# Weight gradient on one core: X of the first slices on SP's queue and slice 0 of G on ACT's, an uneven rounding split, and a last bank in two pieces

## The chip, the cores and the metric

The kernel runs on one core of a Trainium2 chip. The metric is device time in microseconds (us). One profiled execution of each kernel gives a span (first to last instruction), which lies about 1.8 us below the device time of the same execution. PE is TensorE (matmul), PEld its weight loads, DVE VectorE, ACT ScalarE, POOL GpSimd, SP SyncE.

## The reference

```python
batch, m, k, n = 16, 512, 1024, 768
# input: (16, 512, 1024) fp32, grad_output: (16, 512, 768) fp32
grad_weight = np.einsum('bmk,bmn->kn', input, grad_output)
```

With batch and m joined this is one product X^T G: 8192 rows are summed, in 64 slices of 128 rows.

## The kernel before

GpSimd's queue loads X and G slice by slice and casts them to bf16 on the way. The first slices can't wait for that: SP and ACT load slice 0 of G and slices 0 and 1 of X as fp32, and DVE and ACT round them to bf16. G's 768 columns are used in two parts: the "wide" 512 columns as moving operand (steps A and B of the order, four banks each), and the "narrow" 256 columns as stationary operand (steps N). A bank is one accumulator of 128 x 512 fp32 that matmuls write; in the order below the number is the slice up to which a step works, and "!" means that its banks are then copied or added out. Ten long and two short matmuls on constants keep TensorE busy until the data are there.

```python
ORDER = ("A1! B1 N1 B2! N2 A2 N3! ... A50! B50! N64!").split()
WARMUP = [512] * 10 + [128] * 2
...
nc.sync.dma_start(out=gf[:, 0:NA], in_=G[0:P, 0:NA])       # wide G, 256 KB
nc.scalar.dma_start(out=xf[0], in_=X[0:P, :])              # X slice 0, 512 KB
nc.sync.dma_start(out=gf[:, NA:N], in_=G[0:P, NA:N])       # narrow G, 128 KB
nc.scalar.dma_start(out=xf[1], in_=X[P : 2 * P, :])        # X slice 1, 512 KB
...
round_by("DVE", g0, gf, 0, 256)
round_by("ACT", g0, gf, 256, NA)
round_by("DVE", xs[0], xf[0], 0, P)
round_by("ACT", xs[0], xf[0], 2 * P, 4 * P)
round_by("DVE", xs[0], xf[0], P, 2 * P)
...                                              # the rest of X slice 0
def add_slice(part, i, s, first, last):
    ...
    if part.first:
        copy_out(dst, bank, i)                   # even i on DVE, odd on ACT
        if s == 0 and i == 0:
            round_by("DVE", g0, gf, NA, N)       # the narrow G
...
for k in range(KS):                              # the last slices, bank by bank
    pieces = [(0, NA)] if k < KS - 1 else [(0, 256), (256, 384), (384, NA)]
    for c0, c1 in pieces:
        ...                                      # 14 matmuls, then the add
        W = NB if k < 6 else c1 - c0
        for c in range(c0, c1, W):
            nc.sync.dma_start(out=OUT[:, k, c : c + W], in_=acc[:, k, c : c + W])
```

## Time and profile before

| | before |
|---|---|
| device time, median of 3 runs | 176.05 us (175.82 to 176.11) |
| span of the profiled run | 174.3 us |
| PE busy | 97% |
| first real weight load | 5.32 us |
| first N weight load | 6.98 us |
| last add | 171.50 us |

A line of a timeline reads: start (us), length (us), engine, line of the program, operation, what it writes and reads, form, count; in brackets the idle time before it and what ended it. A weight load normally runs one matmul ahead. The lines that carry this part are in the prediction.

### The profile page before, as it was taken

Reading aid. Unit: us, or ns where it says so; the run is one execution under the profiler, and the core shown is the slowest. Engines: PE = TensorE matmul, PEld = TensorE weight load, DVE = VectorE, ACT = ScalarE, POOL = GpSimd, SP = SyncE. Lnnn points to the kernel's source line nnn. Section 1 sums busy time; section 2 is a strip of 40 time slices with the busy share of each in tenths; the row PEclk is TensorE's granted clock in tenths of the full one; section 3 lists DMA queues with packets and bytes.
Section 4 is the critical chain, followed back from the end, with each engine's and each line's share of the span. In section 5 each row is a group of like instructions: output and inputs, shape, how many; then the busy total and the mean of one; then the engine's idle time right before and its main releaser. Section 6 shows DMA issues by size and latency. Waiting matters only on the chain.

```text
span 174.3 us, 2013 instructions
## 1 busy us (share of the span) xinstructions
PE 169.9 (97%) x793; PEld 78.4 (45%) x808; DVE 61.3 (35%) x103; ACT 6.2 (4%) x12; POOL 66.7 (38%) x129
## 2 busy tenths in 40 slices
PE   8999999999999999999999999999999999999993
PEld 3444444444444444444444444444444444444463
DVE  0655582883940039300000662200560003931122
ACT  2640000000000000000000000000000000000000
POOL 7444434444444444444444444444274200000000
PEclk9999999999999999999999999999999999999999
DMA  5999999999999999999999999999999990085623
GB/s 192 276 208 209 207 209 208 208 208 209 207 208 209 207 208 210 207 209 209 206 209 208 208 210 207 207 209 208 207 209 209 207 202 11 0 190 160 170 86 120
DMA packets 25048, 33.35 MB, mean 191 GB/s; under 512 B 6480, under 2 KB 16592, under 8 KB 25040
## 3 DMA queue, kind: packets, MB, share of 16 engines
q0 software_dynamic: 18000, 28.65, 89.9%
q10 hardware_dynamic: 4448, 2.10, 4.7%
q1 hardware_dynamic: 2592, 2.49, 4.2%
q8 instruction: 6, 0.10, 0.2%
q14 instruction: 2, 0.02, 0.0%
HBM read 58.72 MB, written 3.15 MB: 355 GB/s over the span
## 4 chain that ended last, share of the span: by engine, by line
PE 97%; issue 0%; DVE 0%
PE bank L127 63%; PE bank L134 32%; PE bank L81 3%; DVE acc L118 0%
## 5 line engine op out<-in xcount | busy, mean ns | idle before, releaser
L127 PE MATMUL bank<-gt,xt 128*128 128x512 bf16 (+2 forms) x515 | 108.3, 367 | 0.5
L127 PEld LDWEIGHTS <-xt 128*128 128x128 bf16 x524 | 50.2, 98 | 57.2
L118 DVE TENSOR_TENSOR acc<-bank,acc 128x512 f32<-128x512 f32 (+2 forms) x62 | 37.9, 667 | 73.4 <-PE bank L127 72.9
L134 PE MATMUL bank<-xt,gt 128*128 128x512 bf16 x242 | 54.8, 379 | 0.3
L97 POOL DMA_DIRECT2D xt<-in_input_dram x62 | 33.1, 533 | 38.7 <-DMA xt<-in_input_dram 36.5
L92 POOL DMA_DIRECT2D gt<-in_grad_output_dram x63 | 33.8, 536 | 31.2 <-DMA gt<-in_grad_output_dram 24.9
L134 PEld LDWEIGHTS <-gt 128*128 128x128 bf16 x252 | 24.6, 98 | 29.7
L118 DVE TENSOR_TENSOR acct<-bank,acct 128x512 f32<-128x512 f32 x24 | 15.7, 682 | 30.0 <-PE bank L134 29.9
L81 PE MATMUL bank<-const-bfloat16-1.0 128*128 128x512 bf16 (+1 forms) x12 | 4.6, 574 | 0.8 <-PEq L263 0.8
L81 PEld LDWEIGHTS <-const-bfloat16-1.0 128*128 128x128 bf16 x12 | 1.6, 140 | 3.5 <-issue 3.5
L122 DVE COPY acc<-bank 128x512 f32<-128x512 f32 x4 | 2.7, 687 | 1.0 <-PE bank L127 1.0
L180 DVE STREAM_TRANSPOSE turned<-acct 128x512 f32<-128x512 f32 x4 | 2.9, 715 | 0.1
L127 PEld LDWEIGHTS <-x 128*128 128x128 bf16 x16 | 1.6, 98 | 1.9 <-DVE x L107 0.2
L107 DVE CAST g<-gf 128x256 bf16<-128x256 f32 x2 | 0.6, 290 | 4.7 <-DMA gf<-in_grad_output_dram 4.7
L124 ACT COPY acc<-bank 128x512 f32<-128x512 f32 x4 | 2.1, 589 | 1.3 <-PE bank L127 1.3
L127 PE MATMUL bank<-gt,x 128*128 128x512 bf16 x8 | 2.1, 379 | 0.0
L127 PE MATMUL bank<-g,x 128*128 128x512 bf16 x8 | 2.0, 398 | 0.0
L122 DVE COPY acct<-bank 128x512 f32<-128x512 f32 x2 | 1.3, 686 | 1.3 <-PE bank L134 1.3
L107 ACT CAST x<-xf 128x256 bf16<-128x256 f32 x4 | 1.4, 409 | 0.0
L107 ACT ACT_TABLE_LOAD x1 | 1.3, 1283 | 1.7 <-PEq L263 1.7
L124 ACT COPY acct<-bank 128x512 f32<-128x512 f32 x2 | 1.1, 588 | 1.5 <-PE bank L134 1.5
L107 DVE CAST x<-xf 128x256 bf16<-128x256 f32 (+1 forms) x5 | 1.0, 260 | 0.0
(8 smaller groups left out, 3.3 us busy)
## 6 DMA issues: line engine op xcount, KB each, us to landing
xt<-in_input_dram POOLq DMA_DIRECT2D x62, 256.0 KB, 8.5
gt<-in_grad_output_dram POOLq DMA_DIRECT2D x63, 192.0 KB, 8.5
out_dram<-acc SPq DMA_DIRECT2D x13, 128.0 KB, 2.7
xf<-in_input_dram ACTq DMA_DIRECT2D x2, 512.0 KB, 5.1
out_dram<-turned ACTq DMA_DIRECT2D x4, 256.0 KB, 3.4
gf<-in_grad_output_dram SPq DMA_DIRECT2D x1, 256.0 KB, 3.9
out_dram<-acc SPq DMA_DIRECT2D x1, 256.0 KB, 2.0
gf<-in_grad_output_dram SPq DMA_DIRECT2D x1, 128.0 KB, 4.7
```

What stands on the lines that cost most here:

```text
L81: nc.tensor.matmul(wps[:, 0:cols], ones, nc.const_aps.tensor(1.0, (P, cols), bf16), start=True, stop=True,)
L92: nc.gpsimd.dma_start(out=gt, in_=G[s * P : (s + 1) * P, :])
L97: nc.gpsimd.dma_start(out=xs[s], in_=X[s * P : (s + 1) * P, :])
L107: copy(out=dst[:, c0:c1], in_=src[:, c0:c1])
L118: nc.vector.tensor_add(out=dst, in0=src, in1=dst)
L122: nc.vector.tensor_copy(out=dst, in_=src)
L124: nc.scalar.copy(out=dst, in_=src)
L127: nc.tensor.matmul(bank, xs[s][:, k * P : (k + 1) * P], gwide[s][:, c0:c1], start=start, stop=stop)
L134: nc.tensor.matmul(bank, gnarrow[s].rearrange("p (r t) -> p t r", t=NT)[:, t], xs[s][:, h * NA : (h + 1) * NA], start=start, stop=stop,)
L180: nc.vector.transpose(out=turned[:, h * hb : (h + 1) * hb, :, t], in_=dst.rearrange("p (b r) -> p b r", r=SQ),)
```

## The change

Its intent: start X, the larger load, first on SP's queue; let ACT, the slower one, take no X before the first matmul but the larger piece of G; and drop 14 matmuls at the end.

```diff
-    nc.sync.dma_start(out=gf[:, 0:NA], in_=G[0:P, 0:NA])
-    nc.scalar.dma_start(out=xf[0], in_=X[0:P, :])
-    nc.sync.dma_start(out=gf[:, NA:N], in_=G[0:P, NA:N])
-    nc.scalar.dma_start(out=xf[1], in_=X[P : 2 * P, :])
+    nc.sync.dma_start(out=xf[0], in_=X[0:P, :])
+    nc.scalar.dma_start(out=gf[:, 0:NA], in_=G[0:P, 0:NA])
+    nc.sync.dma_start(out=xf[1], in_=X[P : 2 * P, :])
+    nc.scalar.dma_start(out=gf[:, NA:N], in_=G[0:P, NA:N])
...
-    round_by("DVE", g0, gf, 0, 256)
-    round_by("ACT", g0, gf, 256, NA)
+    round_by("ACT", g0, gf, 0, 288)
     round_by("DVE", xs[0], xf[0], 0, P)
+    round_by("DVE", g0, gf, 288, NA)
...
-        pieces = [(0, NA)] if k < KS - 1 else [(0, 256), (256, 384), (384, NA)]
+        pieces = [(0, NA)] if k < KS - 1 else [(0, 384), (384, NA)]
...
-            W = NB if k < 6 else c1 - c0
+            W = NB if k < KS - 1 else c1 - c0
```

## The prediction

> **What bounds the kernel now.** I read the page first: busy shares, then the chain that ended last.
>
> ```profile
> PE 169.9 (97%) x793; PEld 78.4 (45%) x808; DVE 61.3 (35%) x103; ACT 6.2 (4%) x12; POOL 66.7 (38%) x129
> ...
> PE 97%; issue 0%; DVE 0%
> ```
>
> TensorE (PE) is busy for 97% of the span and the chain of waits lies on it from start to end. So the time is: when the first real matmul starts, plus a fixed stream of matmuls, plus what follows the last one. The change touches only the first 6 us and the last 5 us of a 174.3 us span. The middle stays: the waits view has no wait of a matmul on data after the first one. Next, the timeline of the head, from 4.9 to 5.45 us (start, length, engine, line, operation, count, idle time before):
>
> ```profile
> 4.71 0.41 ACT L107 CAST g<-gf 128x256 bf16<-128x256 f32 x1 [1.76 <-DMA gf<-in_grad_output_dram]
> 4.71 0.29 DVE L107 CAST g<-gf 128x256 bf16<-128x256 f32 x1 [4.71 <-DMA gf<-in_grad_output_dram]
> 5.00 0.15 PEld L81 LDWEIGHTS <-const-bfloat16-1.0 128*128 128x128 bf16 x1 [0.28 <-issue]
> 5.04 0.71 ACT L107 CAST x<-xf 128x256 bf16<-128x256 f32 x2
> 5.04 0.56 DVE L107 CAST x<-xf 128x128 bf16<-128x128 f32 x3
> ...
> 5.32 0.10 PEld L127 LDWEIGHTS <-x 128*128 128x128 bf16 x1 [0.17 <-DVE x L107]
> 5.32 0.53 PE L127 MATMUL bank<-g,x 128*128 128x512 bf16 x1
> ```
>
> G of slice 0 is there at 4.71, X at 5.04. DVE rounds its half of G, then the first 128 columns of X, and the first real weight load comes at 5.32, after a wait of 0.17 us for that X. Is X or DVE the later one? Further down the trace a DVE rounding of 256 columns lets the next instruction start 0.20 us later (6.50 to 6.70), so DVE was free at 4.91 and stood until 5.04: **X's landing sets the first matmul**. The view of the tile xf agrees: its two loads take 4.3 and 5.8 us from issue to landing, and 0.74 + 4.3 = 5.04.
>
> How much can an earlier X give? The warm-up's weight loads stand 0.425 us apart, ten matmuls of 512 columns from 0.78 on are done issuing at 5.05, and two of 128 columns at about 0.107 us end near 5.26. The real work comes in the same queue, so it can start at most 0.06 us sooner.
>
> The tail, DVE's timeline from 168.3 us on, and SP's last line:
>
> ```profile
> 168.41 0.69 DVE L118 TENSOR_TENSOR acc<-bank,acc 128x512 f32<-128x512 f32 x1 [2.33 <-PE bank L127]
> 169.94 0.42 DVE L118 TENSOR_TENSOR acc<-bank,acc 128x256 f32<-128x256 f32 x1 [0.84 <-PE bank L127]
> 170.72 0.29 DVE L118 TENSOR_TENSOR acc<-bank,acc 128x128 f32<-128x128 f32 x1 [0.36 <-PE bank L127]
> 171.50 0.29 DVE L118 TENSOR_TENSOR acc<-bank,acc 128x128 f32<-128x128 f32 x1 [0.49 <-PE bank L127]
> ```
>
> ```profile
> 171.82 0.33 SPq L248 DMA_DIRECT2D out_dram<-acc  x1
> ```
>
> Each add starts when its bank is complete. 14 matmuls of 256 columns took 169.94 - 168.41 = 1.53 us (109.3 ns each), 14 of 128 columns 0.78 us (55.7 ns each); a bank of 512 took 168.41 - 165.39 = 3.02 us (215.7 ns each). The last store lands 1.5 us after its issue, at 173.32, and about 1.0 us of closing follows.
>
> **What the Trainium skill says.** "TensorE: Matmul & The Clock Gate", section "Back-to-back issue gap", gives N/2.4 + 2.5 ns for a warm matmul of N columns: 215.8, 109.2 and 55.8. The trace agrees to 0.1 ns; the 131 ns for N=512 that the same section quotes as sustained is not seen here. The same page, "Part 1: The HAM clock gate", says that TensorE runs at half clock until a window of about 3.4 us has been busy. The trace agrees in kind: warm-up matmuls 0.425 us apart, and the first real one starting at 5.32, the second at 5.68 (its end at 6.06 less 0.38), the rest 0.216 apart. 0.36 us for 512 columns is a mixture: t us at 1.2 and 0.36 - t at 2.4 columns per ns give t = 0.29, so the clock opened at about 5.61. "ScalarE: Activation LUTs", section "What ACT_TABLE_LOAD costs", gives 186 + 0.833 N ns for an instruction without pointer operands: 399 at 256 columns against 406 in the trace. "DMA: Bandwidth & Descriptors", section "Issuing engines are not separate DMA queues", says that the choice of issuing engine saves only sequencer time. By that the swap of queues is worth nothing. The trace disagrees a little: the DMA view for 1.8 to 2.1 us, when both loads had been issued at 0.74, shows
>
> ```profile
> q1 hardware_dynamic: 27, 0.06, 92.5%
> q10 hardware_dynamic: 2, 0.01, 19.5%
> ```
>
> q1 is SP's queue (it carries G now, and the 2 MB of the direct output at the end), q10 is ACT's. SP's load moves first, ACT's some 0.3 us later.
>
> **The change, part by part.**
>
> *Queues.* X (512 KB) goes first and G (256 KB) 0.3 us later. From the DMA view, X's 0.52 MB were through at about 4.35 and G's 0.26 MB at about 4.0; each was signalled some 0.7 us later. Between 2.1 and 3.8 us X got about 65% of what both moved (0.35 of 0.54 MB). With X alone until 2.1 us it has 0.07 MB by then and 0.454 left; at 65% it is through when both together have moved 0.70 MB, and G when they have moved 0.26/0.35 = 0.75 MB. Adding up the moved bytes window by window (0.54 MB by 3.8, 0.63 by 4.0, 0.70 by 4.2, 0.77 by 4.4) gives X through at 4.2 and G at 4.35: landings near 4.85 to 4.9 for X, 0.15 to 0.2 us sooner than now, and 4.95 for G, 0.25 later. These are estimates from those windows.
>
> *Rounding.* ACT takes G 0:288 (0.406 + 32 x 0.00083 = 0.43 us), from 4.95 to 5.38. DVE takes 128 columns of X at 4.88 (the next starts 0.14 us later, as three starts from 5.04 to 5.32 show), then G 288:512, 224 columns, between the 0.22 us of 128 and the 0.285 of 256 columns: 0.27 us, from about 5.02 to 5.29. A step from end of rounding to use costs 0.06 (5.26 to 5.32). The first matmul has both operands at about 5.44. Its weight load needs only X and is done by then, which before came after 5.32 and costs 0.10; so compare 5.44 with 5.42: **a slip of 0.02 us**, or, if X lands no sooner than now (5.04 + 0.14 + 0.27 + 0.06 = 5.51), of 0.09. All of this lies before the clock opens at about 5.61, where a lost us costs only half: 0.01 to 0.05 us. Later roundings (128 columns of X by DVE done at about 5.43, the pair by ACT near 5.8) are before their matmuls (second at 5.7, third at 5.9), though the third is close: one more slip of up to 0.1 is possible there.
>
> *Tail.* The last bank becomes 14 x (384/2.4 + 2.5 = 162.5 ns) + 14 x 55.7 = 2.275 + 0.780 = 3.055 us in place of 1.53 + 0.78 + 0.78 = 3.09: **0.035 us less**, the fixed 2.5 ns of 14 matmuls. The new add of 384 columns, between 0.425 and 0.692, is 0.56 us, from 170.69 to 171.25; the last add starts at 171.465, so DVE is free. The store of 384 columns is issued at 171.28 and holds SP for 0.33, to 171.61; the last is issued at 171.79, so SP is free too. The 192 KB need about 0.55 us at the 350 GB/s of the big stores, some 0.8 after issue, so from 172.05 to 172.6, just when the last 64 KB begin: at most 0.05 us of rub. The seventh bank's store split in two goes out at 169.13 and 169.5, long before. Last landing 173.28 to 173.33.
>
> Sum: head +0.01 to +0.05 (to +0.1 with the third matmul late), tail -0.035 to 0. Together about +0.02 us, 0.01% of 176.05. I put the time at 176.05.
>
> **Rivals.** *X on SP really frees the head.* If X and G both land before 4.8, the roundings end before the warm-up does, and the matmul starts at 5.26: 0.06 us at half clock, 0.03, plus 0.035 of the tail. For it: X has the whole queue first. Against it: both loads share the same bytes and about 400 GB/s from 3 us on. It would make 175.98. *DVE becomes the wait.* X now stands ahead of G in DVE's queue; if X lands late, G waits behind it with its data long there: 5.51 or later, some 176.1 to 176.15. *The clock opens later.* The gap between warm-up and real work grows from about 0.1 to 0.2 us. If that falls foul of the busy window, the array stays at half clock for up to 3.4 us more and loses half of that, 1.7 us: 177.7. Against it: the gap is 5% of a window that is otherwise full. *The last stores collide*: 0.05 to 0.2 us, 176.1 to 176.25; for it, 192 KB are 0.51 us ahead of the last 64 on the same queue where 64 KB were 0.78 ahead before.
>
> **Range and chances.** The first, second and fourth rivals stay within 0.2 us; the runs before span 0.29 us by themselves, more than any of these. So the range is run-to-run noise plus 0.1 on each side: 175.65 to 176.45. 2% is 3.5 us, and even the late clock reaches only half of it. Same: 0.98; faster and slower 0.01 each.
>
> **What would show it.** In the profile after: X landing at about 4.85 and G at about 4.95; the first real weight load before 5.2 and its matmul held by ACT's rounding of G, not by DVE's of X; the second matmul at 5.68 to 5.75; 14 matmuls of 384 columns 162.5 ns apart (the add of the 384 piece 2.275 us after that of the seventh bank); the last add 3.055 us after that of the seventh bank; the last landing about 1.5 us after its issue. Wrong would be: a third window at half clock, a wait of TensorE above 0.3 us in the head, or a last store that takes over 1.7 us to land.

## The result, and the profile after

The changed kernel takes **176.49 us** (median of 6 runs, 176.37 to 176.56) against 176.06 us for the kernel before (6 runs, 175.81 to 176.32). The ratio is 1.0025, 95% interval 1.0013 to 1.0038. A ratio here is the mean time of one kernel's fast runs over that of the other's of the same rounds, so it is not quite the ratio of the medians. The change is within 2%, as predicted, but 0.04 us above the range, and the loss of 0.25% is clear of noise.

The profiled span is 174.60 us against 174.27: 0.33 more. The chain that ended last of the changed kernel, its pieces between 0.7 and 7.6 us (start, length, what):

```profile
0.74 4.22 DMA gf<-in_grad_output_dram
...
4.99 0.44 ACT g L107
...
5.47 2.09 PE bank L127 x8
```

A load of G now stands on the chain where before it was TensorE alone. In this execution it is the wide G, issued at 0.74, which the first matmul needs. The head of the changed kernel, from its timeline for 4.4 to 5.5 us:

```profile
4.81 0.31 DVE L107 CAST x<-xf 128x128 bf16<-128x128 f32 x1 [4.81 <-DMA xf<-in_input_dram]
4.99 0.43 ACT L107 CAST g<-gf 128x288 bf16<-128x288 f32 x1 [2.04 <-DMA gf<-in_grad_output_dram]
4.99 0.28 DVE L107 CAST g<-gf 128x224 bf16<-128x224 f32 x1
...
5.31 0.26 PEld L127 LDWEIGHTS <-x 128*128 128x128 bf16 x2 [0.17 <-DVE g L107]
...
5.47 0.58 PE L127 MATMUL bank<-g,x 128*128 128x512 bf16 x1
```

X came at 4.81 and the wide G at 4.99; the first matmul started at 5.47, when ACT had rounded its 288 columns. So far this is what was forecast, though the first matmul of the kernel before had started at 5.32, so that the slip is 0.15 us and not 0.02. The next stretch was not forecast. First the kernel before, its timeline for 6.3 to 8.3 us:

```profile
6.50 0.28 DVE L107 CAST g<-gf 128x256 bf16<-128x256 f32 x1
6.70 0.68 DVE L122 COPY acc<-bank 128x512 f32<-128x512 f32 x1
6.98 0.75 PEld L134 LDWEIGHTS <-g 128*128 128x128 bf16 x4
...
7.85 0.53 PEld L127 LDWEIGHTS <-x 128*128 128x128 bf16 x3
```

and the same stretch of the changed kernel:

```profile
7.02 0.29 DVE L107 CAST g<-gf 128x256 bf16<-128x256 f32 x1 [0.24 <-DMA gf<-in_grad_output_dram]
7.23 0.68 DVE L122 COPY acc<-bank 128x512 f32<-128x512 f32 x1
...
7.36 0.35 PEld L134 LDWEIGHTS <-g 128*128 128x128 bf16 x3 [0.30 <-DVE g L107]
...
7.96 0.10 PEld L134 LDWEIGHTS <-g 128*128 128x128 bf16 x1 [0.26 <-issue]
8.18 0.10 PEld L127 LDWEIGHTS <-x 128*128 128x128 bf16 x1
```

The rounding of the **narrow G** waited for its load until 7.02, the first weight load made of it waited for the rounding until 7.36, and the fourth came only at 7.96, just after the end of the copy behind that rounding, 7.23 + 0.68 = 7.91. The first weight load of step B2 (a slice-1 X block) is at 8.18 against 7.85: 0.33 later. From there to the end of the span both take 166.42 us. **The whole difference of the two profiles lies before 8.2 us.**

A wait of a weight load is not yet a loss, since the load has a matmul's time to spare; the starts of the matmuls count. The N matmuls start at 7.20, 7.41, 7.63 and 7.84 before, and at 7.39, 7.61, 7.96 and 8.18 after. The first of them comes 0.21 us behind the last B1 matmul in both, so its 0.19 us are the later first matmul and the later clock (below). The third is held:

```profile
7.96 0.38 PE L134 MATMUL bank<-x,g 128*128 128x512 bf16 x1
```

By the kernel's order of banks it writes to the third bank of step A1, which DVE's copy behind the late rounding has just freed. So the late narrow G cost 0.14 of the 0.33 us in this execution; how much it costs in others, the experiments show.

Which load is late? Part 6 of each page, KB and us from issue to landing, before:

```profile
gf<-in_grad_output_dram SPq DMA_DIRECT2D x1, 256.0 KB, 3.9
...
gf<-in_grad_output_dram SPq DMA_DIRECT2D x1, 128.0 KB, 4.7
```

and after:

```profile
gf<-in_grad_output_dram ACTq DMA_DIRECT2D x1, 256.0 KB, 4.2
...
gf<-in_grad_output_dram ACTq DMA_DIRECT2D x1, 128.0 KB, 5.8
```

The wide G takes 0.3 us longer, the narrow G 1.1 us longer. The DMA view shows how they moved (queue, packets, MB, share of the 16 engines). Before, 4.0 to 4.8 us, the narrow G is on q1:

```profile
q10 hardware_dynamic: 64, 0.20, 62.2%
q1 hardware_dynamic: 119, 0.12, 41.0%
```

After, 4.4 to 6.0 us, it is on q10, beside X of slice 1 on q1:

```profile
q1 hardware_dynamic: 107, 0.42, 67.0%
...
q10 hardware_dynamic: 94, 0.10, 17.6%
```

Before, nearly all of the narrow G moved in 0.8 us; after, 0.10 MB of it took 1.6 us. In that stretch the two queues moved about equally many packets, but a packet of the view is one row, of the narrow G 1 KB and of X 4 KB. The Trainium skill, "DMA: Bandwidth & Descriptors", section "Queues, rings and completion order", says that each DMA engine takes turns between its queues packet by packet (its packets hold several descriptors, so only the equal turns can be compared). This stretch agrees: 107 packets against 94, 0.42 MB against 0.10. The stretch of before does not: there q1 moved 119 packets to q10's 64.

The packet records of the traces, in which the row size tells the loads apart, show why. Before, the narrow G's rows moved from 4.00 to 5.22 us, and they started just as X of slice 0 ran out on q10 and X of slice 1 began: from 4.2 to 4.6 us 74 of its 128 rows moved beside 20 rows of X. After, its first row moved at 4.53, when X of slice 1 was in full flow, and its last at 6.47; from 4.6 to 6.0 us 89 of its rows moved beside 85 of X. So the narrow G both started 0.5 us later and then had to take turns with longer rows. e8 below tests the sharing itself.

The tail, DVE from 168 us on, in the changed kernel:

```profile
168.74 0.69 DVE L118 TENSOR_TENSOR acc<-bank,acc 128x512 f32<-128x512 f32 x1 [2.33 <-PE bank L127]
171.02 0.56 DVE L118 TENSOR_TENSOR acc<-bank,acc 128x384 f32<-128x384 f32 x1 [1.58 <-PE bank L127]
171.80 0.29 DVE L118 TENSOR_TENSOR acc<-bank,acc 128x128 f32<-128x128 f32 x1 [0.22 <-PE bank L127]
```

From the seventh bank's add to the last one are 3.06 us in place of 3.09. But from the last add to the end of the span are 174.60 - 171.80 = 2.80, against 174.27 - 171.50 = 2.77. The tail comes out even.

### The profile page after: what moved, and what is told of

Its sections match the earlier page's. It is cut to its first block, busy times and chain, and to the rows that moved or that the text cites. A ratio compares the mean times of both kernels' runs of the same rounds, so it can differ in the third digit from the quotient of the medians.

```text
span 174.6 us, 1983 instructions
## 1 busy us (share of the span) xinstructions
PE 170.1 (97%) x779; PEld 77.6 (44%) x794; DVE 61.3 (35%) x102; ACT 6.2 (4%) x12; POOL 66.5 (38%) x129
## 4 chain that ended last, share of the span: by engine, by line
PE 95%; DMA 2%; issue 1%; ACT 0%; DVE 0%
PE bank L127 63%; PE bank L134 32%; DMA gf<-in_grad_output_dram 2%; ACT g L107 0%; DVE acc L118 0%
## 5 line engine op out<-in xcount | busy, mean ns | idle before, releaser
L127 PEld LDWEIGHTS <-xt 128*128 128x128 bf16 x510 | 49.4, 98 | 58.0
L134 PE MATMUL bank<-x,g 128*128 128x512 bf16 x4 | 1.2, 378 | 0.0
```

Source lines behind the costliest of these rows:

```text
L127: nc.tensor.matmul(bank, xs[s][:, k * P : (k + 1) * P], gwide[s][:, c0:c1], start=start, stop=stop)
L134: nc.tensor.matmul(bank, gnarrow[s].rearrange("p (r t) -> p t r", t=NT)[:, t], xs[s][:, h * NA : (h + 1) * NA], start=start, stop=stop,)
```

## The experiments

Ten kernels ran, in three groups, each group on one chip with its own runs of the kernel before. Two numbers beside the ratio are needed to read them. One is when the narrow G was there. The other is when TensorE's clock opened: nine of the twelve traces have a record of the stretch at full clock, and I give its start from the start of the span. (The PEclk row of the page shows 9 throughout and does not show this, as it counts time without such a record as full clock; the spacing of weight loads does show it, 0.42 us before and 0.216 after.) "Late" means that the trace has no such record and the loads are still 0.3 to 0.4 us apart at about 6.1. From the first B2 matmul to the end of the span all take 166.2 us (e1 0.2 more, see there), so that column is what an execution's head cost.

| kernel | narrow G there | clock opens | first N load | first B2 load | first B2 matmul | span | ratio to before (95%) | median |
|---|---|---|---|---|---|---|---|---|
| before | 5.9 | 5.63 | 6.98 | 7.85 | 8.06 | 174.27 | | 176.06 |
| after | 7.02 | 5.91 | 7.36 | 8.18 | 8.39 | 174.60 | 1.0025 (1.0013 to 1.0038) | 176.49 |
| e0_same | 6.6 | 4.80 | 6.98 | 7.80 | 8.01 | 174.20 | 1.0000 (0.9986 to 1.0015) | 176.10 |
| e1_tail | 5.8 | 3.81 | 6.86 | 7.72 | 7.93 | 174.34 | 1.0003 (0.9989 to 1.0018) | 176.08 |
| e2_queues | 7.03 | late | 7.38 | 8.19 | 8.40 | 174.60 | 1.0021 (1.0008 to 1.0034) | 176.51 |
| e3_round | 5.8 | 5.09 | 7.01 | 7.87 | 8.09 | 174.29 | 1.0005 (0.9991 to 1.0019) | 176.11 |
| e4_narrow | 5.6 | late | 7.28 | 8.14 | 8.36 | 174.58 | 0.9999 (0.9986 to 1.0013) | 176.00 |
| e5_fill | 7.36 | 4.86 | 7.71 | 8.56 | 8.73 | 174.94 | 1.0028 (1.0015 to 1.0040) | 176.53 |
| e6_gap | 5.8 | late | 7.42 | 8.28 | 8.49 | 174.70 | 1.0001 (0.9988 to 1.0013) | 175.96 |
| e7_narrow_fill | 5.5 | 4.81 | 6.84 | 7.70 | 7.92 | 174.13 | 1.0000 (0.9986 to 1.0013) | 175.92 |
| e8_x1_last | 5.0 | 5.20 | 6.78 | 8.90 | 8.90 | 175.13 | 1.0056 (1.0039 to 1.0072) | 177.00 |
| e9_copy_first | 7.18 | 3.62 | 7.53 | 8.19 | 8.40 | 174.59 | 1.0015 (1.0003 to 1.0027) | 176.34 |

Where no engine waited for the narrow G, its time is issue plus landing time. One sum explains most rows. With the narrow G there at time t, its rounding lets DVE's copy start 0.21 us later, the copy takes 0.68, the third N matmul starts 0.05 after it, and the first B2 matmul two matmuls (0.43) after that: t + 1.37 us at the earliest. The four profiles in which this copy held the third N matmul, or came to the same time as the clock did, agree: after, e0, e2 and e5 lie 1.37 to 1.38 us behind t. In the others without a wait for a load the clock and the first matmul set the time, 7.92 to 8.49.

**First group: which part of the change costs?** My theory was the late narrow G, brought by the swap of queues. The rivals were the rounding order, and the clock.

### e0_same: the kernel before, as a control

No edit.

> The kernel before, once more, as a control. Theory 'phase': the clock of TensorE opens at a time that changes from execution to execution, so this profile may show an opening away from 5.63 us by some tenths and a third weight load of real work away from 5.69. Theory 'gap': the opening is tied to what TensorE did, so it comes at 5.63 +- 0.05 again. Both: ratio 1.000 +- 0.001, span 174.3 +- 0.15.

The ratio is 1.0000. The clock opened at 4.80, 0.83 us earlier than in the first profile of the same program: the opening is a matter of chance, which speaks for "phase". The span gained only 0.07. In this execution the narrow G also happened to be late (6.6), and with the early clock it was waited for: an earlier clock shows the wait behind it. By the packet records 123 of its 128 rows had moved by 5.0 us, and the last five came one by one until 5.95.

### e1_tail: only the last bank's pieces

```diff
-        pieces = ... else [(0, 256), (256, 384), (384, NA)]
+        pieces = ... else [(0, 384), (384, NA)]
-            W = NB if k < 6 else c1 - c0
+            W = NB if k < KS - 1 else c1 - c0
```

> Only the last bank in 384 + 128 and the seventh bank's store in two. All theories: from the add of the seventh bank to the last add 3.055 us in place of 3.09, last store landing 1.5 to 1.6 us after issue, ratio 0.9998 (0.9990 to 1.0005). If the stores rub, over 1.0005.

The ratio is 1.0003, no difference that can be told. The last add came 3.06 us after the seventh bank's (168.48 to 171.54), the end of the span 2.80 after it. All seven profiles with two pieces (after, e1, e4, e5, e7, e8, e9) have 2.78 to 2.81 there, and all five with three (before, e0, e2, e3, e6) 2.75 to 2.77. So with two pieces the end comes 0.04 us later behind the last add, and the 0.035 saved on matmuls is gone again. That the last store now stands behind 192 KB is the likely reason; it was not tested alone. This profile lost another 0.2 us at 30.6 us, where PE came to a slice of X before its load did (its timeline there):

```profile
30.57 0.55 PEld L127 LDWEIGHTS <-xt 128*128 128x128 bf16 x4 [0.52 <-DMA xt<-in_input_dram]
```

### e2_queues: only the swap of the queues

The first block of the diff above, nothing else.

> Only the swap of the queues. Theory 'late narrow G' (the last third of G lands at 7.0 us, 1.1 later than before, because it now stands behind the wide G, which itself starts later, and beside X of slice 1): the rounding of the narrow G waits for its DMA until 7.0 again, the first N matmul is 0.3 later than before, span 174.55 to 174.7, ratio 1.002 to 1.003. Rival 'rounding order' (X ahead of G on DVE is what costs): narrow G waits but most of the loss is gone, ratio below 1.001.

```profile
7.03 0.30 DVE L107 CAST g<-gf 128x256 bf16<-128x256 f32 x1 [0.22 <-DMA gf<-in_grad_output_dram]
...
7.38 0.69 PEld L134 LDWEIGHTS <-g 128*128 128x128 bf16 x4 [0.17 <-DVE g L107]
```

The ratio is 1.0021, so the swap alone carries the loss. That rests on the five timed runs (176.37 to 176.57), not on this profile. The timeline again shows the wait for the narrow G, and the span is that of the changed kernel, but the clock was late here: the N matmuls start at 7.54, 7.75, 7.97 and 8.19, evenly behind those of B1. The clock alone would have given about this span, as e4's 174.58 shows, and the third N matmul's 7.97 is just when the copy set it free as well.

### e3_round: only the new rounding order

The second block of the diff alone.

> Only the unequal rounding in the new order, with X still on ACT and landing at 5.04. Theory 'late narrow G': no wait for the narrow G, but DVE rounds X at 5.04 and G after it, first matmul at about 5.5, loss 0.1 to 0.2 by itself, ratio 1.0005 to 1.0012. Rival 'rounding order': ratio 1.002 or more.

The ratio is 1.0005, not clear of 1. No engine waits for the narrow G. The first real weight load comes at 5.47, 0.15 later than before, because DVE now rounds G behind X. That is a small cost at most (an estimate: 0.15 us are 0.09% of the time, and at half clock half of that); the rival that it carries the loss falls.

**Second group: is it the narrow G or the clock?** In the profile after the clock opened at 5.91, in that of before at 5.63. I wanted to know whether the longer pause of TensorE before the first real matmul had put it off.

### e4_narrow: the changed kernel, narrow G second on SP

```diff
-    nc.sync.dma_start(out=xf[1], in_=X[P : 2 * P, :])
-    nc.scalar.dma_start(out=gf[:, NA:N], in_=G[0:P, NA:N])
+    nc.sync.dma_start(out=gf[:, NA:N], in_=G[0:P, NA:N])
+    nc.scalar.dma_start(out=xf[1], in_=X[P : 2 * P, :])
```

> The changed kernel with the narrow G second on SP and X of slice 1 second on ACT. Theory 'late narrow G': it lands near 6.0, its rounding by DVE no longer waits, the N matmuls start as soon as the eight wide ones are through, and about 0.13 us of the 0.33 us of span come back: span about 174.45, ratio to before 1.0012 to 1.002. Rival (all of the loss is the later first matmul and the clock): span 174.6, ratio 1.0025.

The ratio is 0.9999: all of the loss is gone, not the 0.13 of 0.33 us I had expected. (The 0.13 was right for the first two profiles, see the third N matmul above; in the timed runs the late narrow G costs more.) The five runs fall into two lots, 175.90 to 176.00 and 176.34 to 176.40. The profiled one is of the second lot, with a late clock, which is why its span of 174.58 looks like no gain.

### e5_fill: the changed kernel with more warm-up

```diff
-WARMUP = [512] * 10 + [128] * 2
+WARMUP = [512] * 10 + [128] * 4
```

> The changed kernel with two more warm-up matmuls of 128 columns, so that TensorE has work until about 5.47, when the first real matmul is ready. Theory 'gap' (the pause of 0.2 us between warm-up and real work put off the opening of the clock from 5.63 to 5.91): it opens at about 5.63 again, the third real weight load comes at 5.75 or so in place of 5.85, and 0.1 to 0.15 us come back: ratio 1.0016 to 1.002. Theory 'phase': no change beyond chance, ratio 1.0025.

The ratio is 1.0028: nothing came back that can be seen, so "gap" falls as the cause of the 0.25%. The clock opened at 4.86, TensorE was early, and its timeline shows it standing for the narrow G:

```profile
7.36 0.29 DVE L107 CAST g<-gf 128x256 bf16<-128x256 f32 x1 [0.92 <-DMA gf<-in_grad_output_dram]
...
7.71 0.33 PEld L134 LDWEIGHTS <-g 128*128 128x128 bf16 x3 [0.98 <-DVE g L107]
```

Here the chain that ended last runs through the narrow G, issued at 1.18, and its rounding:

```profile
1.18 6.15 DMA gf<-in_grad_output_dram
...
7.36 0.30 DVE g L107
```

The last B1 matmul started at 6.84 and the first N matmul at 7.71, 0.87 us apart in place of 0.21; before the third N matmul another 0.14 went to the copy.

### e6_gap: the kernel before with a longer pause

```diff
-WARMUP = [512] * 10 + [128] * 2
+WARMUP = [512] * 10
```

> The kernel before without its two short warm-up matmuls, so that TensorE pauses from about 5.05 to 5.32. Theory 'gap': the clock opens some 0.3 us later, about 5.9, the stream starts 0.1 to 0.15 later, ratio 1.0006 to 1.001. Theory 'phase': the clock opens at 5.63 +- the scatter of the control, ratio 1.000.

The ratio is 1.0001. The profiled run (176.47) did have a late clock, but the other four runs are at 175.89 to 176.15; a pause that put off the clock as a rule would have shown in them. "Gap" falls here too as the cause of the loss. A tenth of a per cent, which it forecast in e6 and e5, lies inside both intervals and is not excluded by the ratios alone.

### e7_narrow_fill: both mends

e4_narrow and e5_fill together.

> Both mends on the changed kernel: narrow G second on SP, two more short warm-up matmuls. If narrow G and gap are both causes and add up: span about 174.35, ratio 1.0003 to 1.001. If only narrow G is: as e4_narrow.

```profile
6.35 0.28 DVE L107 CAST g<-gf 128x256 bf16<-128x256 f32 x1
...
6.84 0.74 PEld L134 LDWEIGHTS <-g 128*128 128x128 bf16 x4
```

The median is 175.92 us against 176.53 for e5_fill on the same chip. Both profiles have nearly the same clock (4.81 and 4.86) and the same warm-up; only the queues of the narrow G and of X of slice 1 differ. The first N load is 0.87 us earlier and the span 0.81 shorter. That is the narrow G's price in this pair, with an early clock; by the medians it is 0.61 us (e5's profiled run is the slowest of its five). Against the kernel before the ratio is 1.0000: it has the lowest median but is not told apart from it.

**Third group: why is the narrow G late, and what does its place in DVE's queue add?**

### e8_x1_last: the changed kernel, X of slice 1 third on ACT

```diff
-    nc.sync.dma_start(out=xf[1], in_=X[P : 2 * P, :])
     nc.scalar.dma_start(out=gf[:, NA:N], in_=G[0:P, NA:N])
+    nc.scalar.dma_start(out=xf[1], in_=X[P : 2 * P, :])
```

> The changed kernel with X of slice 1 moved from second on SP to third on ACT, behind the narrow G; everything of slice 0 stays where the change put it. Theory 'shared with X' (the narrow G, in 1 KB rows, runs beside the 4 KB rows of X of slice 1 and so gets a small share from 4.4 to 6.4 us): it lands at 5.6 to 6.0, DVE does not wait for it, ratio to before 0.999 to 1.001. Rival 'late start' (it is late because the wide G in front of it is 0.3 late, or because ACT's queue is the slower one): it still lands at 6.5 or later, DVE waits, ratio 1.0015 or more.

The theory was right that it lands early (5.0, sooner than its 5.6 to 6.0) and wrong on the time. The narrow G, still second on ACT behind the wide G, took 3.8 us to land instead of 5.8 and was there at 5.0; with no X beside it its 128 rows moved from 4.00 to 4.60. So X of slice 1 beside it made it late, not ACT's queue or the later start of the wide G. But that X now came last, and the timeline shows the next wait in its place:

```profile
6.78 0.74 PEld L134 LDWEIGHTS <-g 128*128 128x128 bf16 x4
...
8.55 0.50 DVE L107 CAST x<-xf 128x256 bf16<-128x256 f32 x2 [1.37 <-DMA xf<-in_input_dram]
8.90 0.55 PEld L127 LDWEIGHTS <-x 128*128 128x128 bf16 x4 [1.37 <-DVE x L107]
```

The ratio is 1.0056. Both loads are wanted early, and the order decides which one is missed.

### e9_copy_first: the narrow G's rounding behind DVE's second copy

```diff
-            if s == 0 and i == 0:
+            if s == 0 and i == 2:
                 round_by("DVE", g0, gf, NA, N)
```

> The changed kernel with DVE's rounding of the narrow G put behind its copy of the third bank, so that the copy no longer waits behind a rounding whose data are late. If the blocked copy is a large part of the loss (the fourth N weight load came 0.26 us after the third in the profile after): the N matmuls run without that pause and the ratio falls to 1.001 to 1.0018. If the landing of the narrow G alone is the floor: the first N matmul comes at 7.4 to 7.7 as before and the ratio stays at 1.002 to 1.003.

```profile
7.18 0.29 DVE L107 CAST g<-gf 128x256 bf16<-128x256 f32 x1 [0.33 <-DMA gf<-in_grad_output_dram]
...
7.53 0.55 PEld L134 LDWEIGHTS <-g 128*128 128x128 bf16 x4 [0.99 <-DVE g L107]
```

Both expectations hold in part. The four N loads now come in one run, and from the first N matmul to the first B2 matmul are 0.87 us (7.53 to 8.40), against 1.00 in the changed kernel and 1.02 in e5_fill: the blocked copy cost 0.13 to 0.15. The ratio of 1.0015 lies where that theory put it, though its interval overlaps the changed kernel's. But the first N load stays at 7.53, though the clock opened as early as 3.62: the landing remains the floor.

## Why the prediction was wrong

**What held.** X and the wide G landed at 4.81 and 4.99 (forecast: about 4.85 and 4.95), the first matmul started at 5.47 (5.44) when ACT's rounding of G was done, the last bank took 3.06 us (3.055), and the end came 0.04 us later behind the last add (a rub of at most 0.05). The sum for the tail, -0.035 to 0, came out at its upper end.

**The step that failed** is "The middle stays: the waits view has no wait of a matmul on data after the first one." The view was of the kernel before, where the narrow G had landed at 5.9 and its rounding at 6.50 had 0.6 us to spare. I worked out landings for the first load of each queue only. The swap changes four loads; the second ones were taken to follow as before, and the narrow G is missing from my list of later roundings and from the rivals. Its landing moved from 5.9 to 7.0 (7.36 in e5_fill), beyond the spare time, and with it the earliest start of the first B2 matmul, t + 1.37, to 8.39 and later, against 7.92 to 8.09 in the profiles with all loads on time and the clock not late. The swap alone (e2) brings the wait and the loss; the one load back on SP (e4, e7) takes the loss away; X of slice 1 taken from its side (e8) makes it land at 5.0.

**A second step was mis-stated:** "All of this lies before the clock opens at about 5.61, where a lost us costs only half." The opening is not a property of the kernel. It came at 4.80 and 5.63 in two executions of the same program, and between 3.62 and later than 6.1 in all profiles. The 0.33 us between the two first profiles is therefore partly chance, and the ratios, not the two spans, decide. The rival "the clock opens later" fell as the cause of the loss (e5, e6).

**A term of the head was mis-sized as well.** "so compare 5.44 with 5.42" adds 0.10 us for a weight load to the 5.32 of before. But from the first matmul to the second there were 0.37 us before (5.32 to 5.69) and 0.38 after (5.47 to 5.85), so that load was no extra cost, and the slip was 0.15 us in place of 0.02. That is 0.07 us of lost work at half clock and 0.15 with the clock open, an estimate, and e3, which has the same slip, shows no loss clear of noise.

**Why the range missed.** I took the noise of the kernel before, from three runs, and added 0.1 on each side. But the late landing is a floor, and a floor takes the good runs away: with the narrow G late the span was 174.60 with a late clock (e2) and 174.59 with the earliest (e9, which also has the freed copy), while with it on time it was 174.58 late (e4) and 174.13 early (e7). The changed kernel's six runs spread over 0.19 us, the eleven runs of before in the first group over 0.61 (175.86 to 176.47). That the clock's phase makes most of the spread of the timed runs is inferred from the profiles; single timed runs have no trace here. Not settled is why the narrow G's landing itself differs between executions of the same queue order, 7.02 to 7.36 with the swap and 5.8 to 6.6 without.

**Forecasts of smaller weight that missed.** The first real weight load came at 5.31, not before 5.2: it waited for DVE's rounding of G, although it needs only X (the releaser in its line). The second matmul came at about 5.85, not 5.68 to 5.75, with the clock open only at 5.91. And none of the three signs of being wrong that the prediction named appeared: no third window at half clock, a longest wait of a real weight load of 0.30 us in the head (not above 0.3), and a last store that landed after 1.6 us (not over 1.7). They did not watch the step that failed.

## What to carry to other kernels

When loads change queues, work out the landing and the first use of every load on those queues, not only of the first in each; the slack of the later ones is not in a view of waits. Judge a late operand by the starts of the matmuls, not by the wait of a weight load. A small load with 1 KB rows lost out beside a large one with 4 KB rows, so look at what runs beside it and which of the two is used first. And when several limits lie within some tenths of a us, an improvement of one shows only in the runs in which the others are late.

## What the Trainium skill lacked or had wrong

- "DMA: Bandwidth & Descriptors", section "Issuing engines are not separate DMA queues", says that loads issued by different engines share the same DMA engines, but not that it matters which load runs beside which; that the swap is worth nothing was the prediction's own conclusion from it. Here the pairing of loads on two queues moved one landing by 1.1 us (4.7 to 5.8 us after issue) and the kernel's time by 0.25%. Nor does its section "Queues, rings and completion order" draw the consequence of equal turns that short rows lose (89 rows of 1 KB beside 85 of 4 KB from 4.6 to 6.0 us).
- The same page has nothing on a lag of ACT's queue: with both loads issued at 0.74, SP's moved 27 packets (of G) and ACT's 2 (of X) between 1.8 and 2.1 us; after the swap it was 9 (of X) and none (of G).
- "TensorE: Matmul & The Clock Gate", part 1, gives the opening of the clock as varying by 500 ns from run to run. With an almost unchanged warm-up it lay between 3.62 and later than 6.1 us, at least 2.5 us apart. The note in the same part, by which one kernel ran 6, 11 or 14 matmuls at the slow clock, fits better: at 0.425 us each, the spacing here, 6 to 14 are 3.4 us apart (an estimate from the page's counts). Its window of 3413 ns agrees: in all nine traces with a record the full-clock stretch is 170.67 us, 50 windows.
